# One level of Strassen's scheme for both products of an MLP, in a hybrid decoder block on one core

## The chip, the cores and the metric

The kernel runs on one core of a Trainium2 chip. The metric is device time in microseconds (us) of one execution, as the median of several runs. The core's engines are TensorE (matmuls and transposes, PE in the profile, its weight loads PEld), VectorE (DVE), ScalarE (ACT), GpSimd (POOL) and SyncE (SP), which issues most DMAs. Each engine takes its own instructions in their order and waits for others by semaphores.

## The reference, cut to what matters

One decoder layer on 1,024 positions of width 1,024, all in float32: a mixer of an SSD scan and an attention, then an MLP with squared ReLU, both with residuals. The change touches the MLP and the two norms around it.

```python
def reference(x, ...):                      # x (1, 1024, 1024)
    h = x + hybrid_mixer(rmsnorm(x, norm_mix_w), ...)
    u = square(relu(rmsnorm(h, norm_mlp_w) @ w_up))     # w_up (1024, 4096)
    h = h + u @ w_down                                   # w_down (4096, 1024)
    return rmsnorm(h, norm_final_w)
```

## The kernel before

A product of two float32 operands is made of three matmuls of the type fp32r: each operand a is split into a high part (a rounded copy) and a low part (a minus the copy), and high x high, high x low and low x high are summed in one PSUM bank. A bank holds 128 x 512 values; the pools `d`, `s`, `t` and `v` have 2, 3, 2 and 1 of them (line 105). SBUF tiles come from pools with fixed numbers of buffers (line 103); a tile that is made anew waits until the buffer's last reader is done. A scheduler sets the order on each engine, except while an engine's key is in `kept`, when its instructions keep the order in which they are written.

After the output projection, whose last part adds its result onto the residual tiles `h1` (eight of 128 x 1024), come two stages. The second norm (line 1142) takes four row tiles at a time: ScalarE squares and sums them, GpSimd makes the factor (`rstd_of`), VectorE scales, and `norm_transpose` (line 198) turns them on TensorE and splits them into `gh` (ScalarE) and `gl` (VectorE), eight tiles each, model width on partitions, all 1,024 positions.

The MLP runs over 16 chunks of two 128-wide blocks of the inner width (`FC = 2`). `mlp_up` (line 1163) loads and splits a block of `w_up` (GpSimd the high part, VectorE the low) and, for each half of the positions, sums 8 x 3 matmuls of 128 x 512 in one bank `pu`; ScalarE applies the ReLU, GpSimd squares, ScalarE and VectorE split the result into `uu`. `mlp_wd` (line 1190) splits the rows of `w_down`. `mlp_down` (line 1200) makes for each of 8 row tiles and 2 column halves 6 matmuls into a bank `pn`, which VectorE adds onto `h1`. The loop at the end calls the up products of chunk c + 1 before the down products of chunk c:

```python
    us = mlp_up(0)
    for c in range(NCH):
        wd = mlp_wd(c)
        nxt = mlp_up(c + 1) if c + 1 < NCH else None
        mlp_down(c, us, wd)
        us = nxt
```

So up and down products alternate, a chunk being 96 + 96 matmuls, and squared activations never leave SBUF. In the last chunk `final` and `store` (lines 1224 and 1243) make the final norm of each row tile as it is completed.

## Time and profile before

| | us |
|---|---|
| median of 3 runs | 1755.26 |
| lowest and highest run | 1750.23, 1757.10 |
| the profiled execution's span | 1752.7 |

The profiled execution is one run, observed by the hardware; times of single instructions are from it. Its mean granted TensorE clock is 0.986 of full speed. A page of it has six parts: busy time by engine, forty slices of the span, DMA queues, the chain of work that ended last, the costliest groups of instructions, and DMA issues. The trace behind it can be asked for a timeline, for waits, and for sums over windows. "Busy" time of matmuls overlaps, since one begins before the one ahead of it has left the array; the distance from start to start is the price of one in a stream. The MLP with the second norm stands from about 1032 to 1743 us, the final norm's rest behind it.

### The profile page before, as it was taken

The numbers are of one execution on the slowest core, as the hardware profiler recorded it, in microseconds if no ns is written. First come the engines' busy times: TensorE is split into PE (matmuls) and PEld (weight loads), VectorE is DVE, ScalarE is ACT, GpSimd is POOL, SyncE is SP. The second block draws the span as 40 slices with busy tenths as digits, with TensorE's granted clock in tenths as the row PEclk, the third lists the DMA queues.
The fourth block names the chain that finished last, engine by engine and source line by source line (L and its number), as shares of the span: only waits on it lengthen the run. The fifth ranks groups of instructions, "written<-read, shape, count | busy, mean of one in ns | idle before, by whom it ended". The sixth has DMA issues, their size and how long they took to land.

```text
span 1752.7 us, 22604 instructions
## 1 busy us (share of the span) xinstructions
PE 1696.3 (97%) x8378; PEld 1416.5 (81%) x8378; DVE 1021.6 (58%) x1959; ACT 550.6 (31%) x1277; POOL 527.1 (30%) x731
## 2 busy tenths in 40 slices
PE   7999898899999999999999999999999999999997
...
DMA packets 142134, 108.23 MB, mean 62 GB/s; under 512 B 41060, under 2 KB 125240, under 8 KB 142024
## 3 DMA queue, kind: packets, MB, share of 16 engines
...
q0 software_dynamic: 1024, 0.53, 0.1%
...
## 4 chain that ended last, share of the span: by engine, by line
PE 78%; DMA 6%; DVE 4%; ACT 3%; issue 3%; POOL 2%; POOLq 0%; DVEq 0%; ACTq 0%; SPq 0%
PE pu L85 19%; PE pn L85 19%; PE po L85 10%; PE pj_qk L85 9%; PE pj_v L85 5%; DMA eb<-cum_d 5%; PE s L85 4%; PE o L85 4%; PE tp L85 3%; PE pj_x L85 3%; ACT eb L85 2%; DVE acc_x L85 1%; PE pj_c L85 1%; PE pb L85 0%; PE pv L85 0%
## 5 line engine op out<-in xcount | busy, mean ns | idle before, releaser
L85 PE MATMUL pn<-wh_dn,uu 128*128 128x512 f32 x1024 | 318.8, 390 | 2.5 <-POOL wh_dn L85 2.4
L85 PEld LDWEIGHTS pn<-wh_dn,uu 128*128 128x128 f32 x1024 | 192.8, 188 | 43.4 <-POOL wh_dn L85 3.2
L85 DVE TENSOR_TENSOR h<-h,pn 128x512 f32<-128x512 f32 x256 | 167.7, 680 | 93.0 <-PE pn L85 92.7
L85 PE MATMUL pn<-wl_dn,uu 128*128 128x512 f32 x512 | 199.8, 391 | 0.0
L85 PE MATMUL pu<-gh,wh_up 128*128 128x512 f32 x512 | 199.7, 390 | 0.0
L85 PE MATMUL pu<-gl,wh_up 128*128 128x512 f32 x512 | 199.6, 390 | 0.0
L85 PE MATMUL pu<-gh,wl_up 128*128 128x512 f32 x512 | 199.4, 389 | 0.0
L85 ACT ACTIVATE u<-pu 128x512 f32<-128x512 f32 x64 | 38.3, 599 | 500.4 <-PE pu L85 500.4
L85 POOL TENSOR_SCALAR p<-p,rs 128x512 f32<-128x512 f32 (+2 forms) x144 | 102.8, 719 | 247.1 <-DVE rs L85 135.5
L85 PE MATMUL po<-wh_o,yy 128*128 128x512 f32 x512 | 161.8, 393 | 1.2 <-DVE k L85 1.2
L85 POOL TENSOR_TENSOR u<-u 128x512 f32<-128x512 f32 x64 | 67.9, 1060 | 256.7 <-ACT u L85 256.6
L85 ACT ACTIVATE p<-s,mx 128x512 f32<-128x512 f32 (+1 forms) x192 | 110.2, 578 | 89.8 <-DVE mx L85 69.6
L85 DVE TENSOR_TENSOR uu<-u,uu 128x512 fp32r<-128x512 f32 x64 | 44.1, 689 | 159.6 <-ACT uu L85 159.3
L85 DVE TENSOR_TENSOR pl<-tp,ph 128x512 fp32r<-128x512 f32 x192 | 105.9, 552 | 39.8 <-ACT ph L85 36.8
L85 POOL TENSOR_SCALAR wh_up<-ws_up 128x512 fp32r<-128x512 f32 x64 | 38.5, 619 | 271.6 <-DMA ws_up<-in_w_up_dram 140.0
L85 ACT CAST ph<-tp 128x512 fp32r<-128x512 f32 x192 | 91.5, 477 | 70.9 <-PE tp L85 70.5
L85 PEld LDWEIGHTS pn<-wl_dn,uu 128*128 128x128 f32 x512 | 96.6, 189 | 20.1
L85 PEld LDWEIGHTS pu<-gh,wh_up 128*128 128x128 f32 x512 | 96.1, 188 | 20.0 <-ACT gh L85 0.3
L85 PEld LDWEIGHTS pu<-gh,wl_up 128*128 128x128 f32 x512 | 96.1, 188 | 20.0 <-DVE wl_up L85 0.2
L85 PEld LDWEIGHTS pu<-gl,wh_up 128*128 128x128 f32 x512 | 96.1, 188 | 19.7
L85 PEld LDWEIGHTS po<-wh_o,yy 128*128 128x128 f32 x512 | 95.5, 188 | 20.0 <-DVE k L85 1.5
L85 DVE TENSOR_TENSOR wl_dn<-wsd,wh_dn 128x512 fp32r<-128x512 f32 x64 | 57.9, 909 | 84.3 <-POOL wh_dn L85 84.3
...
## 6 DMA issues: line engine op xcount, KB each, us to landing
ws_up<-in_w_up_dram SPq DMA_DIRECT2D x32, 512.0 KB, 4.2
wsd<-in_w_down_dram SPq DMA_DIRECT2D x32, 512.0 KB, 3.5
eb<-cum_d SPq DMA_DIRECT2D x16, 512.0 KB, 8.9
...
wso<-in_w_out_dram SPq DMA_DIRECT2D x16, 512.0 KB, 3.5
...
wsz<-in_w_in_dram SPq DMA_DIRECT2D x10, 512.0 KB, 3.7
x<-in_x_dram SPq DMA_DIRECT2D x8, 512.0 KB, 5.1
```

The source lines that it names most:

```text
L85: i = call(*args, **kw)
```

## The change

Both products of the MLP are written as 2 x 2 blocks and made by Strassen's scheme in Winograd's form: seven block products on sums and differences of blocks (s1 to s4 and a11, a12, a22 of the left operand, t1 to t4 and b11, b21, b22 of the right), whose results are summed into four output blocks. Sums are made in float32 before the split into high and low parts.

- **Second norm.** The normalised rows are four blocks: model width halves by position halves. `norm_rows` also stores `h1` to DRAM (`h1_d`), since its tiles are needed for others. The first half of the positions gives b11 and b21 and plain copies of both (`cc`); then a11 and a12 of the first pair are multiplied; the second half gives t1 to t4 and b22, made from the transposes and `cc`. TensorE's order is as written from there on.
- **Up stage.** It runs over 16 pairs of 128-wide inner blocks. `up_split` makes the seven left operands of a pair, with three sums on GpSimd and one on VectorE; ScalarE makes each high part, VectorE each low one. A product is 4 x 3 matmuls of 128 x 512. Three banks serve a pair, and two of them are read and then accumulated further: after s2 b is read, s3 is added, b is read, and so on. The four output blocks are passed through ReLU and square (ScalarE), GpSimd makes the four sums that are the left operands of the next product, and all seven go to DRAM (`uc_d`).
- **Down stage.** It begins after the whole up stage: eight chunks of two pairs, each of four slots i (row tiles i and i + 4). `down_in` loads the seven 128 x 128 blocks of a slot and pair, ScalarE makes the high part (128 x 896), GpSimd the low one (VectorE for i = 3). Inputs of a slot are asked for two slots ahead. `down_split` makes the seven right operands of a pair from `w_down`, with four sums on GpSimd. `down_mm` makes seven products of 6 matmuls; after each, VectorE adds the bank onto a quarter of `h1` or onto a sum `acc`, which the last chunk adds onto three quarters. `h1` is loaded again from DRAM before the stage.

```diff
+    h1_d = dp.tile([T, D], F32, name="h1_d")
...
+            sy.dma_start(out=h1_d[tt * P:(tt + 1) * P, :], in_=h1[tt])
...
+    def parts(o, src, low_by):
+        ac.copy(o[:, 0], src)
+        low_by.tensor_tensor(out=o[:, 1], in0=src, in1=r32(o[:, 0]), op=ALU.subtract)
+    cc = []
+    nts = norm_rows(0)
+    for k in range(HK):
+        cc.append(sb("q", [P, 2, 512], F32, f"cc{k}"))
+        for i, m in enumerate(("b11", "b21")):
+            kk = k + HK * i
+            pt = turn(nts, kk, 0)
+            quarter(m, k, pt, mlpw(kk))
+            ac.activation(cc[k][:, i, :], pt, AF.Copy, scale=mlpw(kk))
...
+    def up_prod(bank, p, m, b, first):
+        o = uop[p][m + "o"]
+        n = 0
+        for k in range(HK):
+            g = gq[b][k]
+            for x, y in ((0, 0), (0, 1), (1, 0)):
+                n += 1
+                te.matmul(
+                    bank, o[:, x, k, :], g[:, y, :], start=first and n == 1, stop=n == 3 * HK,
+                    skip_group_check=True,
+                )
...
+    uc_d = [dp.tile([P, 4, 7, P], F32, name=f"uc_d{p}") for p in range(NPAIR)]
...
+    def up_first(p):
+        a = banks[p, "a"] = ps("d", f"pu_a{p}")
+        up_prod(a, p, "a11", "b11", True)
+        t1s[p] = sb(("y", "y", "vt")[p % 3], [P, 512], F32, f"ut1_{p}")
+        ac.copy(t1s[p], a)
+    def up_second(p):
+        up_prod(banks[p, "a"], p, "a12", "b21", False)
+    def up_rest(p, between):
+        a = banks[p, "a"]
+        t1 = t1s[p]
+        st = [sb(("p", "p", "ws")[(4 * p + j) % 3], [P, 4, 2, P], F32, f"uc{p}_{j}") for j in range(4)]
...
+        b = ps("s", f"pu_b{p}")
+        up_prod(b, p, "s2", "t2", True)
+        u2 = tmp("u2")
+        ve.tensor_tensor(out=u2, in0=b, in1=t1, op=ALU.add)
+        if between is not None:
+            between()
+        ac.activation(view("a11"), v3(a), AF.Relu)
+        ac.activation(view("a11"), view("a11"), AF.Square)
+        up_prod(b, p, "s3", "t3", False)
+        u3 = tmp("u3")
+        ve.tensor_tensor(out=u3, in0=b, in1=t1, op=ALU.add)
+        c = ps("t", f"pu_c{p}")
+        up_prod(c, p, "s1", "t1", True)
+        ve.tensor_tensor(out=u3, in0=c, in1=u3, op=ALU.add)
+        up_prod(b, p, "a22", "t4", False)
+        ac.activation(u3, u3, AF.Relu)
+        ac.activation(view("a22"), v3(u3), AF.Square)
+        c21 = tmp("c21")
+        ve.tensor_tensor(out=c21, in0=b, in1=t1, op=ALU.add)
+        ac.activation(c21, c21, AF.Relu)
+        ac.activation(view("a12"), v3(c21), AF.Square)
+        up_prod(c, p, "s4", "b22", False)
+        ve.tensor_tensor(out=u2, in0=c, in1=u2, op=ALU.add)
+        act(u2, u2)
+        a21 = v3(u2)
+        gp.tensor_tensor(out=view("s3"), in0=view("a11"), in1=a21, op=ALU.subtract)
+        gp.tensor_tensor(out=view("s1"), in0=a21, in1=view("a22"), op=ALU.add)
+        gp.tensor_tensor(out=view("s2"), in0=view("s1"), in1=view("a11"), op=ALU.subtract)
+        gp.tensor_tensor(out=view("s4"), in0=view("a12"), in1=view("s2"), op=ALU.subtract)
+        for j in range(4):
+            n = min(2, 7 - 2 * j)
+            sy.dma_start(out=uc_d[p][:, :, 2 * j:2 * j + n, :], in_=st[j][:, :, 0:n, :])
...
+    up_split(0, ("a11", "a12"))
+    kept.add("t")
+    up_first(0)
+    up_second(0)
+    kept.discard("t")
+    nts = norm_rows(1)
+    pts = {}
+    kept.add("t")
...
+    for k in range(HK):
+        w1, w2 = mlpw(k), mlpw(k + HK)
+        p12 = turn(nts, k, 1)
+        c12 = sb("t", [P, 512], F32, f"c12_{k}")
+        ac.activation(c12, p12, AF.Copy, scale=w1)
+        ta = sb("ws", [P, 2, 512], F32, f"ta{k}")
+        ve.scalar_tensor_tensor(
+            out=ta[:, 0, :], in0=p12, scalar=w1, in1=cc[k][:, 0, :], op0=ALU.mult, op1=ALU.subtract
+        )
+        p22 = turn(nts, k + HK, 1)
+        ve.scalar_tensor_tensor(
+            out=ta[:, 1, :], in0=p22, scalar=w2, in1=ta[:, 0, :], op0=ALU.mult, op1=ALU.subtract
+        )
+        parts(gtile("t2", k), ta[:, 1, :], ve)
+        tb = [sb("t", [P, 512], F32, f"tb{k}_{j}") for j in range(2)]
+        ve.scalar_tensor_tensor(
+            out=tb[0], in0=p22, scalar=w2, in1=c12, op0=ALU.mult, op1=ALU.subtract
+        )
+        parts(gtile("t3", k), tb[0], ve)
+        quarter("b22", k, p22, w2)
+        parts(gtile("t1", k), ta[:, 0, :], gp)
+        gp.tensor_tensor(out=tb[1], in0=cc[k][:, 1, :], in1=ta[:, 1, :], op=ALU.subtract)
+        parts(gtile("t4", k), tb[1], gp)
+    for p in range(1, PRE):
+        up_split(p, ("a11", "a12"))
+        up_first(p)
+        up_second(p)
+    for p in range(NPAIR):
+        if p < PRE:
+            up_split(p, ("s2", "s3", "s1", "a22", "s4"))
+            up_rest(p, None)
+        else:
+            up_load(p)
+            up_split(p, ORDER)
...
+        def out(m):
+            tag = "w" if nd[0] % 22 < 6 else "hT"
+            nd[0] += 1
+            o = sb(tag, [P, 2, 512], F32R, f"do_{m}_{p}")
+            parts(o, src[m], ve)
+            dop[p, m] = o
+        out("b11")
+        add("t1", b12, b11, ALU.subtract)
+        out("t1")
+        add("t3", b22, b12, ALU.subtract)
+        out("t3")
+        add("t2", b22, src["t1"], ALU.subtract)
+        out("t2")
+        out("b21")
+        out("b22")
+        add("t4", b21, src["t2"], ALU.subtract)
+        out("t4")
...
+    def down_in(c, i):
+        for p in range(c * CP, (c + 1) * CP):
+            tag = "pq"[nu[0] % 8 // 4]
+            nu[0] += 2
+            lo = sb(tag, [P, 7, P], F32R, f"ul{p}_{i}")
+            hi = sb(tag, [P, 7, P], F32R, f"uh{p}_{i}")
+            sy.dma_start(out=r32(lo), in_=uc_d[p][:, i])
+            ac.copy(hi, r32(lo))
+            (gp if i % 4 < 3 else ve).tensor_tensor(out=lo, in0=r32(lo), in1=r32(hi), op=ALU.subtract)
+            us_in[p, i] = hi, lo
...
+    def down_mm(c, i):
+        last = c == NCH - 1
+        def prod(bank, m, b, first):
+            j = UM.index(m)
+            n, total = 0, 3 * CP
+            for p in range(c * CP, (c + 1) * CP):
+                w = dop[p, b]
+                for x, y in ((0, 0), (0, 1), (1, 0)):
+                    n += 1
+                    te.matmul(
+                        bank, us_in[p, i][x][:, j, :], w[:, y, :], start=first and n == 1,
+                        stop=n == total, skip_group_check=True,
+                    )
+        def read(bank, dst):
+            ve.tensor_tensor(out=dst, in0=dst, in1=bank, op=ALU.add)
+        h11, h12 = h1[i][:, 0:512], h1[i][:, 512:]
+        h21, h22 = h1[i + 4][:, 0:512], h1[i + 4][:, 512:]
+        nm = f"{c}_{i}"
+        ba = ps("d", f"pn_a{nm}")
+        prod(ba, "a11", "b11", True)
+        read(ba, h11)
+        bb = ps("s", f"pn_b{nm}")
+        prod(bb, "s1", "t1", True)
+        read(bb, h22)
+        bc = ps("t", f"pn_c{nm}")
+        prod(bc, "s3", "t3", True)
+        read(bc, h22)
+        prod(ba, "s2", "t2", False)
+        if c == 0:
+            acc[i] = sb("p0", [P, 512], F32, f"acc{i}")
+            ac.copy(acc[i], ba)
+        else:
+            read(ba, acc[i])
+        if last:
+            for dst in (h22, h12, h21):
+                gp.tensor_tensor(out=dst, in0=dst, in1=acc[i], op=ALU.add)
+        bd = ps("v", f"pn_d{nm}")
+        prod(bd, "a12", "b21", True)
+        read(bd, h11)
+        prod(bb, "s4", "b22", False)
+        read(bb, h12)
+        if last:
+            final(i)
+        prod(bc, "a22", "t4", False)
+        read(bc, h21)
+        if last:
+            final(i + 4)
...
+    for p in range(CP):
+        down_load(p)
+        down_split(p)
+    h1 = {}
+    for i in range(4):
+        for tt in (i, i + 4):
+            h1[tt] = sb("q", [P, D], F32, f"h1b_{tt}")
+            sy.dma_start(out=h1[tt], in_=h1_d[tt * P:(tt + 1) * P, :])
+        if i < 2:
+            down_in(0, i)
+    wfb = sb("ws", [P, D], F32, "wfb")
+    sy.dma_start(out=wfb, in_=norm_final_w.partition_broadcast(P))
+    slots = [(c, i) for c in range(NCH) for i in range(4)]
+    for n, (c, i) in enumerate(slots):
+        if c + 1 < NCH and i % 2 == 0:
+            down_load((c + 1) * CP + i // 2)
+        down_mm(c, i)
+        if n + 2 < len(slots):
+            down_in(*slots[n + 2])
+        if c + 1 < NCH and i % 2 == 1:
+            down_split((c + 1) * CP + i // 2)
```

How the instructions stand. ScalarE at the second norm, before: high parts `gh` and squares of the second half's tiles in turn (`hn4` is row tile 4, the first of the second half).

```order
L85 ACTIVATE gh4_10342<-nt_m_0_4_10410,prm_92 128x512
L85 ACTIVATE gh5_10343<-nt_m_0_5_10417,prm_92 128x512
L85 ACTIVATE gh6_10344<-nt_m_0_6_10424,prm_92 128x512
L85 ACTIVATE hn4_10438,ss_m4_10439<-h1_4_9242 128x1024
L85 ACTIVATE gh7_10345<-nt_m_0_7_10431,prm_92 128x512
L85 ACTIVATE hn5_10445,ss_m5_10446<-h1_5_9310 128x1024
```

And now: high parts, the copies `cc`, a copy of the first bank (`ut1`), and then the squares.

```order
L85 ACTIVATE g_b21_2_10424<-nt_m_0_6_10419,prm_92 128x512
L85 ACTIVATE cc2_10409<-nt_m_0_2_10410,prm_92 128x512
L85 ACTIVATE g_b11_3_10434<-nt_m_0_3_10429,prm_92 128x512
L85 ACTIVATE cc2_10409<-nt_m_0_6_10419,prm_92 128x512
L85 ACTIVATE g_b21_3_10443<-nt_m_0_7_10438,prm_92 128x512
L85 ACTIVATE cc3_10428<-nt_m_0_3_10429,prm_92 128x512
L85 COPY ut1_0_10490<-pu_a0_10477 128x512
L85 ACTIVATE cc3_10428<-nt_m_0_7_10438,prm_92 128x512
L85 ACTIVATE hn4_10504,ss_m4_10505<-h1_4_9242 128x1024
L85 ACTIVATE hn5_10512,ss_m5_10513<-h1_5_9310 128x1024
```

What moved: 17 operations instead of 7 stand ahead of the first square of the second half, and TensorE's transposes of that half, which need those squares' factors, stand behind the first pair's a11 and a12.

SP at the turn from the up to the down stage, which the kernel before does not have. `h1b` are the residual tiles loaded again, `ul0_1` the input of pair 0 for slot 1, `uc_d15` the sums of the last pair on their way to DRAM, `wsd` raw weights.

```order
L85 DMA h1b_0_13097<-h1_d_10338 128x1024
L85 DMA h1b_4_13099<-h1_d_10338 128x1024
L85 DMA h1b_1_13111<-h1_d_10338 128x1024
L85 DMA h1b_5_13113<-h1_d_10338 128x1024
L85 DMA ul0_1_13115<-uc_d0_10447 128x896
L85 DMA uc_d15_10462<-uc15_3_12932 512x1x128
L85 DMA wsd2_0_13135<-in_w_down_dram 128x1024
L85 DMA wfb_13133<-in_norm_final_w_dram 128x1024
L85 DMA ul0_0_13101<-uc_d0_10447 128x896
L85 DMA uc_d15_10462<-uc15_0_12929 512x1x256
L85 DMA uc_d15_10462<-uc15_1_12930 512x1x256
L85 DMA uc_d15_10462<-uc15_2_12931 512x1x256
```

What moved: the first input of the second pair, `ul1_0`, stands behind the last pair's stores and four residual tiles.

VectorE in a stretch of down products, before: low parts of weights (`wl`) and reads of banks onto `h1`.

```order
L85 TENSOR_TENSOR h1_4_9242<-h1_4_9242,pn0_4_0_10884 128x512
L85 TENSOR_TENSOR h1_4_9242<-h1_4_9242,pn0_4_1_10892 128x512
L85 TENSOR_TENSOR h1_5_9310<-h1_5_9310,pn0_5_0_10900 128x512
L85 TENSOR_TENSOR h1_5_9310<-h1_5_9310,pn0_5_1_10908 128x512
L85 TENSOR_TENSOR wl_up4_10967<-ws_up4_10964,wh_up4_10966 128x512 x2
L85 TENSOR_TENSOR h1_6_9378<-h1_6_9378,pn0_6_0_10916 128x512
L85 TENSOR_TENSOR h1_6_9378<-h1_6_9378,pn0_6_1_10924 128x512
L85 TENSOR_TENSOR h1_7_9416<-h1_7_9416,pn0_7_0_10932 128x512
L85 TENSOR_TENSOR h1_7_9416<-h1_7_9416,pn0_7_1_10940 128x512
```

And now, in the last slot of a chunk: `do` are low parts of the weights' operands of the next chunks, `pn` are banks.

```order
L85 TENSOR_TENSOR do_t1_7_14069<-ds_t1_7_14067,do_t1_7_14069 128x512
L85 TENSOR_TENSOR h1b_3_13129<-h1b_3_13129,pn_a2_3_14001 128x512
L85 TENSOR_TENSOR do_t3_7_14074<-ds_t3_7_14072,do_t3_7_14074 128x512
L85 TENSOR_TENSOR h1b_7_13131<-h1b_7_13131,pn_b2_3_14009 128x512
L85 TENSOR_TENSOR do_t2_7_14079<-ds_t2_7_14077,do_t2_7_14079 128x512
L85 TENSOR_TENSOR h1b_7_13131<-h1b_7_13131,pn_c2_3_14017 128x512
L85 TENSOR_TENSOR do_b21_7_14082<-wsd7_1_13936,do_b21_7_14082 128x512
L85 TENSOR_TENSOR acc3_13394<-acc3_13394,pn_a2_3_14001 128x512
L85 TENSOR_TENSOR do_b22_7_14085<-wsd7_1_13936,do_b22_7_14085 128x512
L85 TENSOR_TENSOR h1b_3_13129<-h1b_3_13129,pn_d2_3_14032 128x512
L85 TENSOR_TENSOR do_t4_7_14090<-ds_t4_7_14088,do_t4_7_14090 128x512
L85 TENSOR_TENSOR h1b_3_13129<-h1b_3_13129,pn_b2_3_14009 128x512
```

What moved: between each two reads of banks now stands a subtraction of two SBUF operands, which waits for ScalarE's high part.

## Rows read from the trace of the kernel before

**Rows 1.** The page's first part (busy us, share of the span and instructions of each engine) and TensorE's row of its 40 slices.

```profile
PE 1696.3 (97%) x8378; PEld 1416.5 (81%) x8378; DVE 1021.6 (58%) x1959; ACT 550.6 (31%) x1277; POOL 527.1 (30%) x731
...
PE   7999898899999999999999999999999999999997
```

**Rows 2.** The page's fourth part, the chain that ended last: shares by engine, then by line and tile (pu are the up products, pn the down products).

```profile
PE 78%; DMA 6%; DVE 4%; ACT 3%; issue 3%; POOL 2%; POOLq 0%; DVEq 0%; ACTq 0%; SPq 0%
PE pu L85 19%; PE pn L85 19%; PE po L85 10%; PE pj_qk L85 9%; PE pj_v L85 5%; DMA eb<-cum_d 5%; PE s L85 4%; PE o L85 4%; PE tp L85 3%; PE pj_x L85 3%; ACT eb L85 2%; DVE acc_x L85 1%; PE pj_c L85 1%; PE pb L85 0%; PE pv L85 0%
```

**Rows 3.** The page's fifth part, the matmuls of the MLP: count, busy us, mean ns of one, idle before.

```profile
L85 PE MATMUL pn<-wh_dn,uu 128*128 128x512 f32 x1024 | 318.8, 390 | 2.5 <-POOL wh_dn L85 2.4
...
L85 PE MATMUL pn<-wl_dn,uu 128*128 128x512 f32 x512 | 199.8, 391 | 0.0
...
L85 PE MATMUL pu<-gh,wh_up 128*128 128x512 f32 x512 | 199.7, 390 | 0.0
...
L85 PE MATMUL pu<-gl,wh_up 128*128 128x512 f32 x512 | 199.6, 390 | 0.0
...
L85 PE MATMUL pu<-gh,wl_up 128*128 128x512 f32 x512 | 199.4, 389 | 0.0
```

**Rows 4.** Timeline of TensorE: the first transposes of the second norm, the first up product, two matmuls of the steady stream with 21 others between them, and the last matmul (start us, us, engine, line, operation).

```profile
1031.65 3.48 PE L85 MATMUL nt_m<-ident,hn 128*128 128x128 f32 x28
...
1034.89 0.48 PE L85 MATMUL pu<-gh,wh_up 128*128 128x512 f32 x1
...
1051.02 0.39 PE L85 MATMUL pu<-gh,wh_up 128*128 128x512 f32 x1
...
1056.01 0.39 PE L85 MATMUL pu<-gl,wh_up 128*128 128x512 f32 x1
...
1742.39 0.39 PE L85 MATMUL pn<-wh_dn,uu 128*128 128x512 f32 x1
```

**Rows 5.** TensorE's waits in the window 1030 to 1753, the longest (us in total, times, longest).

```profile
PE pn L85 <- POOL wh_dn L85: 2.4, 1, 2.4
```

**Rows 6.** Windows: length, then busy us (and instructions) of TensorE, its weight loads, VectorE, ScalarE and GpSimd, then TensorE's granted clock, the DMA share and GB/s. First the whole MLP, then the stretch about the wait of rows 5.

```profile
1031.65:1742.78 711.13, 707.49 (x3137) 583.51 (x3135) 327.59 (x468) 103.31 (x181) 158.75 (x219) 1.00 0.16 49
...
1066.00:1068.00 2.00, 0.00 (x0) 0.00 (x0) 0.56 (x1) 0.00 (x0) 0.56 (x1) 1.00 0.03 4
...
1068.00:1070.00 2.00, 1.81 (x5) 1.27 (x6) 1.69 (x2) 0.00 (x0) 0.64 (x2) 0.77 0.00 0
...
1070.00:1075.00 5.00, 5.00 (x19) 3.99 (x18) 2.72 (x5) 0.00 (x0) 0.87 (x2) 0.75 0.37 105
```

**Rows 7.** The page's fifth part, the other engines' operations of the MLP: reads of a bank onto the residual, the low part of the activations, the squaring and the ReLU.

```profile
L85 DVE TENSOR_TENSOR h<-h,pn 128x512 f32<-128x512 f32 x256 | 167.7, 680 | 93.0 <-PE pn L85 92.7
...
L85 DVE TENSOR_TENSOR uu<-u,uu 128x512 fp32r<-128x512 f32 x64 | 44.1, 689 | 159.6 <-ACT uu L85 159.3
...
L85 POOL TENSOR_TENSOR u<-u 128x512 f32<-128x512 f32 x64 | 67.9, 1060 | 256.7 <-ACT u L85 256.6
...
L85 ACT ACTIVATE u<-pu 128x512 f32<-128x512 f32 x64 | 38.3, 599 | 500.4 <-PE pu L85 500.4
```

**Rows 8.** Timeline of VectorE in a stretch of down products: a subtraction with both operands in SBUF, then three reads of banks back to back.

```profile
1399.85 0.68 DVE L85 TENSOR_TENSOR wl_dn<-wsd,wh_dn 128x512 fp32r<-128x512 f32 x1
1400.46 1.87 DVE L85 TENSOR_TENSOR h<-h,pn 128x512 f32<-128x512 f32 x3
```

**Rows 9.** Timeline of GpSimd and VectorE where both work on SBUF at once (other engines' rows left out).

```profile
1081.07 1.20 POOL L85 TENSOR_SCALAR wh_up<-ws_up 128x512 fp32r<-128x512 f32 x2 [5.73 <-DMA ws_up<-in_w_up_dram]
...
1081.72 2.54 DVE L85 TENSOR_TENSOR wl_up<-ws_up,wh_up 128x512 fp32r<-128x512 f32 x2 [4.88 <-POOL wh_up L85]
...
1082.28 1.42 POOL L85 TENSOR_TENSOR u<-u 128x512 f32<-128x512 f32 x1
```

**Rows 10.** Timeline of ScalarE at the second norm: high parts of the first half, then two squares of the second half's tiles.

```profile
1032.29 4.20 ACT L85 ACTIVATE gh<-nt_m,prm 128x512 fp32r<-128x512 f32 x7 [20.27 <-PE nt_m L85]
...
1039.03 1.06 ACT L85 ACTIVATE hn<-h 128x1024 f32<-128x1024 f32 x1
...
1040.07 1.06 ACT L85 ACTIVATE hn<-h 128x1024 f32<-128x1024 f32 x1
```

**Rows 11.** Timeline of VectorE there: low parts of the first half, and the last scaled tile of the second.

```profile
1033.01 4.70 DVE L85 SCALAR_TENSOR_TENSOR gl<-nt_m,prm,gh 128x512 fp32r<-128x512 f32 x7 [0.47 <-ACT gh L85]
...
1043.02 0.75 DVE L85 TENSOR_SCALAR hn<-h,v_m 128x1024 f32<-128x1024 f32 x1 [0.71 <-POOL v_m L85]
```

**Rows 12.** Windows (columns as in rows 6): 4 us in the output projection's loads.

```profile
836.00:840.00 4.00, 2.68 (x13) 1.91 (x13) 3.29 (x13) 2.84 (x9) 0.62 (x2) 1.00 0.92 360
```

**Rows 13.** The page's sixth part, DMA issues: count, KB each, median us from issue to landing.

```profile
ws_up<-in_w_up_dram SPq DMA_DIRECT2D x32, 512.0 KB, 4.2
wsd<-in_w_down_dram SPq DMA_DIRECT2D x32, 512.0 KB, 3.5
```

**Rows 14.** Timeline of the end: VectorE's last products of the final norm and the last output DMA's issue.

```profile
1748.32 1.41 DVE L85 SCALAR_TENSOR_TENSOR fsq<-h,v_f,wfb 128x512 f32<-128x512 f32 x2 [0.71 <-POOL v_f L85]
...
1749.77 0.37 ACTq L85 DMA_DIRECT2D out_dram<-fsq  x1
```

180 lines of the change are left out of this document (92 added, 88 removed).

## Prediction

> **What bounds the kernel now.** I read the page's busy shares first, then the chain of waits, then the stretch that the change touches, by timeline and windows. TensorE is busy 97% of the span [rows 1], and the two MLP products are 38% of the chain that ended last, 19% each [rows 2]. The reader is to see that these products wait for almost nothing: 3,072 matmuls [rows 3], one wait of 2.4 us [rows 5]. So the price of one is its spacing, not its "mean ns", which overlaps its neighbours: from 1051.02 to 1056.01 there are 22 steps, 4.99 / 22 = 0.2268 us each [rows 4]. The stretch from the first transpose of the second norm (1031.65) to the end of the last matmul (1742.39 + 0.39) is 711.1 us [rows 4]. Work in it: 3,072 x 0.2268 = 696.7, and 64 transposes at (1034.89 - 1031.65) / 28 = 0.116, 7.4; together 704.1. **So 7.0 us are lost there now**, 4 of them around the one wait: no matmul in 1066 to 1068, and then a granted clock of 0.77 and 0.75, a mix of 1.2 and 2.4 GHz, costing 0.23 x 2 + 0.25 x 5 = 1.7 [rows 6]. The other engines have room: in this stretch VectorE is busy 328 of 711 us, ScalarE 103, GpSimd 159 [rows 6].
>
> **The gain.** The listing of the changed kernel shows 16 pairs x 7 x 12 = 1,344 matmuls up and 32 slots x 7 x 6 = 1,344 down, all 128x512 with a weight load each, as before. 384 fewer x 0.2268 = **87.1 us less TensorE work**. Everything else below is waiting that this work no longer covers.
>
> **Steady up stage.** A pair takes 84 x 0.2268 = 19.05. VectorE has 5 reads of banks at 0.62 (1.87 / 3) and 8 SBUF operations at 0.61 (1399.85 to 1400.46) [rows 8], 8.0 in all, and 13.3 if each of the 8 takes 2.54 / 2 = 1.27, as beside a busy GpSimd [rows 9]. ScalarE has 16 operations at about 0.60 [rows 7], 9.6. GpSimd has 7 additions at 1.06 [rows 7], 7.4, or 9.9 at 1.42 each [rows 9]. All lie under 19. A bank is read and then accumulated into again, but another product of 12 x 0.2268 = 2.72 lies between, against a read of 0.68 [rows 7] behind at most one subtraction of 1.27: covered. Without that cover each return to a bank would cost about 1.0 (read 0.68 and two handovers); that happens once each in pairs 0 and 1, where `between` is None. **+2**, bounds 0 and 6.
>
> **Start of the MLP.** Here the cover goes. ScalarE now writes, for the first four row tiles, 8 high parts and 8 plain copies `cc` and one copy of a bank before it reaches the squares of the other four tiles: from 1032.29, 17 x 0.60 = 10.2 [rows 10], then squares 1.04 apart. Its last square starts at about 1045.6, against 1040.07 now; 3.7 later (1040.07 to 1043.02 + 0.75) the last scaled tile stands [rows 10, 11]: 1049.3. Then four rounds build t1 to t4 and b22. Each has 6 ScalarE operations of 0.60 and a start-up of two VectorE operations of 0.67 [rows 11] that they wait for, about 4.5; with some pair-0 work between, 20 us. All TensorE has meanwhile is 64 transposes and the a11 and a12 products of pairs 0 and 1, whose b11 and b21 come from the first half. I put the end of s3 of pair 0 at 1074: 72 matmuls (16.3) and 64 transposes (7.4) in 42.6 us leave 19 idle. With one spell of low clock as in [rows 6], 1.7, **+21**. Bounds: 12 (the four rounds run at ScalarE's pace alone, 24 x 0.60 = 14.4, and start where the squares now end) and 27 (half clock through both idle stretches).
>
> **Between up and down.** Before, down products of a chunk followed up products of the next, and no stage ended. Now the first down product needs inputs that come back from DRAM, and the order shows what stands ahead of them. The four input tiles take the buffers of the last pair's sums. After the last up product at T: read 0.68, ReLU, a cast, square 3 x 0.60, three GpSimd sums 3 x 1.06, then on GpSimd a weight sum that waits for its own load, and the fourth sum: T + 8. The write to DRAM, 3.5 as a 512 KB load takes [rows 13], T + 11.7; the load into the freed tile, T + 15; high part of 896 columns 0.60 x 896 / 512 = 1.05, low part on GpSimd 1.06 x 896 / 512 = 1.85: T + 18. A second path: on SP, three 512 KB residual tiles (released only in the last product), three more loads and a write stand ahead of the first input, 3.7 MB; at 360 GB/s, the most that I read in 4 us [rows 12], 10 us. The first half of the inputs can start the products earlier. I take 16, and 1.7 of clock: **+18**, bounds 8 (inputs meet old tiles) and 24.
>
> **Steady down stage.** A slot is 42 matmuls, 9.53; a chunk four slots, 38.1. VectorE per chunk: 28 reads at 0.62, 14 weight subtractions, 2 input subtractions of 896. Alone: 17.4 + 14 x 0.61 + 2 x 1.07 = 28.1. But the order puts all 14 in the last slot of a chunk and the first of the next, one between each two reads: 14 x 1.23 = 17.2 of 19.05 with nothing to slow them. GpSimd has in those two slots 4 input subtractions (1.85) and some 6 sums (1.06), 13.8 of 19.05. What one costs beside the other, the rows show: two subtractions 2.54 while GpSimd's addition takes 1.42 instead of 1.06 [rows 7, 9]. Stepped row by row at 0.9 a subtraction and 0.61 a read, the first read in the second of these slots ends 14.6 after the first slot began; the product that goes into that bank again is due at 9.53 + 3 x 1.36 = 13.6, so TensorE waits some 1.1. Nine subtractions stand ahead of it, so at 1.15 each it waits 3.3. Inputs run on two buffers: load 3.5, casts, two subtractions of 1.85 to 2.5 on GpSimd, 8 to 10 us against 9.53. I take 2.5 for each of 7 boundaries, **+17.5**, nearer [rows 9] than [rows 8], since GpSimd is busy 70% there; bounds 0 and 6 each. In the last chunk two input loads stand on SP behind output stores that wait for the final norm: **+5**, bounds 0 and 8.
>
> The Trainium skill has a rule against this part. Its page "SBUF — State Buffer", section "Who interferes with whom", says that a VectorE instruction with two SBUF inputs and a GpSimd instruction that reads SBUF shut each other out for the whole instruction. The trace agrees: both reach 2.54 and 1.42 in [rows 9], and PSUM reads, with one SBUF input, stay at 0.68 [rows 7]. By it a subtraction can wait out a whole input subtraction of 1.85; where that held for every instruction, the time would be that of the second rival below.
>
> **Tail.** After the last matmul come 9.9 us now (1742.8 to 1752.7) [rows 4, 14]; the new final norm has the same steps with fewer tiles waiting: 0, bounds -2 and +2. Elsewhere nothing moves but eight residual stores and four weight splits inside the output projection, where TensorE does not wait for VectorE now: 0.
>
> **How the numbers follow.** Against the profiled execution: -87.1 - 7.0 + 2 + 21 + 18 + 17.5 + 5 = -30.6, so 1752.7 - 30.6 = 1722. The median of the runs is 2.6 above the profiled span: **1725**. All low bounds together (0 + 12 + 8 + 0 + 0 - 2 = 18) would give 1679, all high ones (6 + 27 + 24 + 42 + 8 + 2 = 109) 1770. Chance of a time near the forecast, 1700 to 1742: 0.60.
>
> **Rivals.**
> 1. *The waits are absorbed.* Raw tiles and sums are fetched a pair ahead, so the boundary slots may cost 0.5 each, the turn 10 and the start 15: 15 + 10 + 4 + 2 = 31, -63, with the 2.6 a time of 1692. For it: GpSimd's sums stand two slots early in the order. Against: ScalarE's 17 operations at the start have no slack. 0.17.
> 2. *VectorE and GpSimd become the bound of the down stage, and the kernel is slower.* If VectorE and GpSimd take turns throughout, a chunk costs 28.1 + 6 x 1.85 + 8 x 1.06 = 47.7 in place of 38.1, +9.6 for 8 chunks = 77 instead of 22.5: -94.1 + 41 + 77 = +24, a time of 1779. It decides from 6.6 us a chunk ((94.1 - 41) / 8), and from 7.7 it is slower by over 0.5%. For it: reads stand in line behind the subtractions. Against: the reads themselves don't slow beside GpSimd [rows 7]. 0.09.
> 3. *The inputs come late in every slot.* If load, casts and two subtractions (up to 11 us) exceed the slot by 1.5, 32 x 1.5 = 48 in place of 22.5: -5, a time of 1750. For it: each load also waits in SP's line behind weight loads. Against: 1.4 MB per slot is 150 GB/s, and 360 were moved in [rows 12]. 0.14.
> That the products are not fewer is excluded by the listing.
>
> Range: 1688 to 1757, which leaves out the slower case and some of the absorbed one. 0.5% (about what a measurement of this kernel can tell from no change) is 8.8 us: faster 0.77 (forecast and first rival), same 0.14 (third), slower 0.09 (second).
>
> **What would show it.** In the profile after: spacing of up products still 0.227 and no waits in the middle of the up stage; a TensorE gap of 15 to 20 us spread over the first 42 us of the MLP, with ScalarE busy throughout; one gap of some 16 us between the last up and the first down product, ended by an input tile; in the down stage waits at chunk boundaries, released by VectorE's reads, and subtractions of 0.9 to 1.2. Wrong would be: a subtraction near 0.7 (rival 1), TensorE waiting in every slot for inputs (rival 3), or VectorE busy nine tenths of the down stage (rival 2).

## The result: slower by 0.9%

| | before | after |
|---|---|---|
| median of 4 runs, us | 1754.03 | 1767.05 |
| lowest and highest | 1750.23, 1757.10 | 1766.85, 1774.25 |
| span of the profiled execution | 1752.7 | 1765.0 |

The ratio is 1.0086, with a 95% interval of 1.0063 to 1.0109. The forecast was 1725, with a range to 1757.

**The profile after.** First the page's busy share of TensorE, its row of slices and the chain (they answer to [rows 1, 2]):

```profile
PE 1632.2 (92%) x7994; PEld 1349.6 (76%) x7994; DVE 1211.0 (69%) x2082; ACT 763.7 (43%) x1610; POOL 779.0 (44%) x788
...
PE   7999898899999999999999968999999599888896
...
PE 63%; DVE 11%; DMA 8%; issue 5%; ACT 5%; POOL 4%; SPq 0%; POOLq 0%; DVEq 0%; ACTq 0%
```

TensorE is 64 us less busy, but its share of the span fell from 97% to 92%, and its share of the chain from 78% to 63%. TensorE's waits from 1030 on (they answer to [rows 5]; us in total, times, longest):

```profile
PE pn_a L85 <- POOL ul L85: 26.7, 16, 5.3
PE pn_a L85 <- DVE h1b L85: 16.5, 10, 2.8
PE pn_a L85 <- ACT uh L85: 14.3, 3, 9.5
```

All three stand before products into the bank pn_a, which opens a down slot and comes back in its middle. `ul` is a low part of the inputs, `h1b` a read onto the residual, `uh` a high part. Windows then show where the time went (they answer to [rows 6]; columns: length, then busy us and instructions of TensorE, weight loads, VectorE, ScalarE, GpSimd, then the granted clock, DMA share, GB/s):

```profile
1027.12:1091.62 64.50, 45.75 (x198) 36.01 (x196) 46.07 (x55) 39.88 (x70) 32.32 (x27) 0.87 0.15 48
1091.62:1366.34 274.72, 274.72 (x1213) 227.29 (x1211) 158.29 (x185) 138.29 (x230) 139.08 (x101) 1.00 0.51 161
1366.34:1410.05 43.71, 23.83 (x85) 17.67 (x85) 38.11 (x32) 17.86 (x29) 40.34 (x24) 0.73 0.64 233
1429.09:1446.68 17.59, 13.23 (x44) 9.72 (x42) 17.59 (x16) 3.18 (x5) 14.09 (x8) 0.81 0.33 112
1446.68:1475.24 28.56, 28.56 (x128) 23.65 (x126) 21.49 (x29) 12.26 (x19) 11.99 (x7) 1.00 0.34 115
1429.09:1703.99 274.90, 242.53 (x1009) 192.54 (x1008) 229.78 (x263) 87.41 (x127) 151.14 (x81) 0.97 0.35 119
1703.99:1753.80 49.81, 44.35 (x169) 34.05 (x167) 26.66 (x40) 18.83 (x39) 36.11 (x39) 0.90 0.35 119
```

In order: the start of the MLP; the rest of the up stage, where TensorE never pauses (1,212 matmuls in 274.72, 0.2267 each); the turn to the third down slot; slot 0 of chunk 1; slots 1 to 3 of chunk 1, again without a pause; chunks 1 to 6 together; chunk 7. So chunk 1 loses its time in its first slot alone. Over chunks 1 to 6, 35.2 of the 46.4 us lost lie in the first slot of a chunk, the rest in the second and third, none in the fourth. With TensorE's work taken off (0.2267 a matmul, 7.4 for the transposes) each term of the sum can be read:

| term | forecast | after |
|---|---|---|
| 384 matmuls fewer | -87.1 | -87.1 |
| losses of before, gone | -7.0 | -7.0 |
| start of the MLP and steady up stage | 21 + 2 | 64.5 - 37.3 = 27.2, and 0 |
| turn | 18 | 43.7 - 19.05 = 24.7 |
| chunks 1 to 6 | 6 x 2.5 = 15 | 274.9 - 228.5 = 46.4 |
| chunk 7 with its boundary | 2.5 + 5 | 49.8 - 38.1 = 11.7 |
| after the last matmul | 0 | +1.3 |
| ahead of the MLP | 0 | -4.5 |
| sum | -30.6 | 12.7 (measured 12.3) |

The -4.5 lies in code that the change leaves alone: the first transposes start at 1027.12 where they stood at 1031.65 [rows 4]. It is no effect of the change that I can show; in the twelve kernels of the experiments they start anywhere from 1026.5 to 1032.0. Without that row and the one above it, the stages exceed the forecast by 46 us, of which 31 are in the six middle chunks.

The same windows also split the loss by kind. TensorE's idle time is a window's length less its busy time: 18.8 at the start, 19.9 at the turn, 32.4 in chunks 1 to 6 and 5.5 in chunk 7. The rest is TensorE busy longer than its work takes at 0.2267 a matmul: 8.4, 4.8, 14.0 and 6.3, together 33.5, where the forecast had two spells of low clock of 1.7 each. Outside chunks 1 to 6 the idle time is 44.1 us for a forecast of 44.5 (19 + 2, 16, and 2.5 + 5).

**One boundary, row by row.** TensorE in slot 0 of chunk 1 (start us, us, operation, count, idle before and what ended it):

```profile
1432.67 0.50 PE L85 MATMUL pn_a<-do_b,ul 128*128 128x512 f32 x1 [2.28 <-POOL ul L85]
...
1434.62 1.05 PE L85 MATMUL pn_c<-do_t,uh 128*128 128x512 f32 x2
...
1435.90 1.05 PE L85 MATMUL pn_c<-do_t,uh 128*128 128x512 f32 x2
...
1439.45 0.74 PE L85 MATMUL pn_a<-do_t,uh 128*128 128x512 f32 x2 [2.07 <-DVE h1b L85]
...
1440.96 1.05 PE L85 MATMUL pn_d<-do_b,uh 128*128 128x512 f32 x2
```

The slot takes 17.59 us for 9.52 of work. TensorE waits 2.28 for a low part of GpSimd's and 2.07 for VectorE's read of the bank that s2 x t2 wants back. Between and behind the waits the matmuls stand 0.43 apart (1434.62 to 1435.90, three in 1.28) where 0.227 is usual: about half the clock. The slot's window shows a granted clock of 0.81, and a window over 1434.20 to 1437.40 alone one of 0.50. So 4.35 of the 8.07 us lost are waits, and 3.7 are slower matmuls behind them. VectorE there:

```profile
1424.36 2.03 DVE L85 TENSOR_TENSOR do_t<-ds_t,do_t 128x512 fp32r<-128x512 f32 x1
...
1428.90 1.78 DVE L85 TENSOR_TENSOR do_t<-ds_t,do_t 128x512 fp32r<-128x512 f32 x1
...
1431.20 1.96 DVE L85 TENSOR_TENSOR do_b<-wsd,do_b 128x512 fp32r<-128x512 f32 x1
...
1439.32 1.39 DVE L85 TENSOR_TENSOR do_b<-wsd,do_b 128x512 fp32r<-128x512 f32 x1
...
1446.26 0.68 DVE L85 TENSOR_TENSOR do_b<-wsd,do_b 128x512 fp32r<-128x512 f32 x1
```

A weight subtraction takes 1.96 to 2.03 beside a low part of GpSimd's, 1.39 to 1.78 beside a weight sum, and 0.68 while GpSimd is idle (1446.26). The reads stand between these subtractions. GpSimd there:

```profile
1421.99 1.29 POOL L85 TENSOR_TENSOR ds_t<-wsd,ds_t 128x512 f32<-128x512 f32 x1 [11.67 <-DVE do_t L85]
...
1430.10 2.52 POOL L85 TENSOR_TENSOR ul<-ul,uh 128x896 fp32r<-128x896 f32 x1
...
1432.57 1.75 POOL L85 TENSOR_TENSOR ds_t<-wsd,wsd 128x512 f32<-128x512 f32 x1
```

The low part that TensorE waits for is made from 1430.10 to 1432.62, though ScalarE had its high part ready at 1426.75. Ahead of it in GpSimd's line stand weight sums that wait for tiles which VectorE's subtractions still read: 11.67 us at 1421.99, then 0.69 and 0.63. The two engines' lines thus hold each other up. In chunks 1 to 6 the groups are:

```profile
L85 DVE TENSOR_TENSOR do_t<-ds_t,do_t 128x512 fp32r<-128x512 f32 x48 | 69.0, 1437 | 3.9 <-ACT do_t L85 3.9
...
L85 DVE TENSOR_TENSOR do_b<-wsd,do_b 128x512 fp32r<-128x512 f32 x35 | 48.8, 1394 | 0.0
...
L85 POOL TENSOR_TENSOR ds_t<-wsd,ds_t 128x512 f32<-128x512 f32 x22 | 29.9, 1358 | 64.1 <-DVE do_t L85 60.5 <-PE pn_c L85 3.5
...
L85 POOL TENSOR_TENSOR ul<-ul,uh 128x896 fp32r<-128x896 f32 x37 | 88.1, 2390 | 44.7 <-ACT uh L85 44.6
```

`do_t` are the weight subtractions on sums, `do_b` those on raw blocks; all 83 together take 1.42 in the mean. TensorE's 32.3 us of waits in these chunks are 18.9 for low parts and 13.4 for VectorE's reads.

The slower matmuls are of two kinds. Chunks 3 to 5 run at a granted clock of 1.00, and still TensorE is busy 118.55 for 114.3 of work there, some 0.3 for each of its 13 waits:

```profile
1521.54:1658.09 136.55, 118.55 (x505) 93.43 (x504) 113.67 (x133) 45.13 (x67) 79.29 (x43) 1.00 0.37 127
```

In chunks 1, 2 and 6 it is busy 9.7 longer than its work; there the granted clock is 0.93 to 0.96.

### The profile page after: what moved, and what is told of

It is laid out like the page before. It is cut to its first block, busy times and chain, and to the rows that moved or that the text cites. A ratio compares the mean times of both kernels' runs of the same rounds, so it can differ in the third digit from the quotient of the medians.

```text
span 1765.0 us, 22987 instructions
## 1 busy us (share of the span) xinstructions
PE 1632.2 (92%) x7994; PEld 1349.6 (76%) x7994; DVE 1211.0 (69%) x2082; ACT 763.7 (43%) x1610; POOL 779.0 (44%) x788
## 4 chain that ended last, share of the span: by engine, by line
PE 63%; DVE 11%; DMA 8%; issue 5%; ACT 5%; POOL 4%; SPq 0%; POOLq 0%; DVEq 0%; ACTq 0%
PE po L85 9%; PE pj_qk L85 8%; PE pu_b L85 7%; PE pj_v L85 5%; DMA eb<-cum_d 5%; PE pu_c L85 5%; PE pu_a L85 4%; PE s L85 4%; PE o L85 3%; PE tp L85 3%; PE pj_x L85 3%; PE pn_a L85 3%; PE pn_b L85 2%; DVE do_t L85 2%; PE pn_c L85 2%
## 5 line engine op out<-in xcount | busy, mean ns | idle before, releaser
L85 POOL TENSOR_TENSOR ul<-ul,uh 128x896 fp32r<-128x896 f32 x48 | 112.9, 2361 | 54.0 <-ACT uh L85 53.7
L85 DVE TENSOR_TENSOR pl<-tp,ph 128x512 fp32r<-128x512 f32 x192 | 105.9, 553 | 38.1 <-ACT ph L85 34.9
L85 PE MATMUL pj_qk<-hh,wl_qk 128*128 128x512 f32 x256 | 106.2, 415 | 0.0
L85 PE MATMUL pj_qk<-hl,wh_qk 128*128 128x512 f32 x256 | 105.9, 414 | 0.0
L85 PE MATMUL pj_qk<-hh,wh_qk 128*128 128x512 f32 x256 | 103.4, 404 | 0.0
L85 PE MATMUL s<-k,q 68*128 68x512 f32 (+7 forms) x384 | 101.9, 347 | 1.1 <-ACT p L85 0.9
L85 PE MATMUL po<-wl_o,yy 128*128 128x512 f32 x256 | 100.6, 393 | 0.0
L85 PE MATMUL pu_b<-g_t,uo_s 128*128 128x512 f32 x384 | 93.9, 394 | 4.0 <-DVE uu L85 4.0
L85 PE MATMUL tp<-ident,p 128*128 128x128 f32 x576 | 95.2, 273 | 1.2 <-POOL p L85 1.2
L85 PE MATMUL pu_a<-g_b,uo_a 128*128 128x512 f32 x384 | 94.5, 396 | 1.4 <-ACT ut L85 1.4
L85 DVE TENSOR_TENSOR do_t<-ds_t,do_t 128x512 fp32r<-128x512 f32 x64 | 91.6, 1433 | 5.6 <-ACT do_t L85 5.5
```

The source lines that it names most:

```text
L85: i = call(*args, **kw)
```

## Experiments

Three theories. **Lock**: VectorE's subtractions (two SBUF operands) and GpSimd's instructions take turns, and these longer durations are the loss. **Burst**: the loss comes from the order; 14 splits stand in two slots, and half of them belong to the chunk after next. **Inputs**: load, casts and two low parts take longer than a slot. VectorE's order in slot 3 of chunk 0 shows what the burst is (`do_t1_3` is the split of block t1 of pair 3, `pn_a0_3` the bank a of chunk 0, slot 3):

```order
L85 TENSOR_TENSOR do_t1_3_13433<-ds_t1_3_13431,do_t1_3_13433 128x512
L85 TENSOR_TENSOR h1b_3_13129<-h1b_3_13129,pn_a0_3_13364 128x512
L85 TENSOR_TENSOR do_b11_4_13587<-wsd4_0_13457,do_b11_4_13587 128x512
L85 TENSOR_TENSOR h1b_7_13131<-h1b_7_13131,pn_b0_3_13372 128x512
L85 TENSOR_TENSOR do_t3_3_13438<-ds_t3_3_13436,do_t3_3_13438 128x512
L85 TENSOR_TENSOR h1b_7_13131<-h1b_7_13131,pn_c0_3_13380 128x512
L85 TENSOR_TENSOR do_t2_3_13443<-ds_t2_3_13441,do_t2_3_13443 128x512
L85 TENSOR_TENSOR do_b21_3_13446<-wsd3_1_13298,do_b21_3_13446 128x512
L85 TENSOR_TENSOR do_t1_4_13592<-ds_t1_4_13590,do_t1_4_13592 128x512
```

Pair 3 is of chunk 1 and urgent; pair 4 is of chunk 2 and needed 38 us later. Tiles of both come free in the same slot, and so both are split there, between the reads.

**e1, the order alone.** `side` holds what stands behind each of a slot's seven reads; `a` and `b` are the next chunk's pairs, and `convert` (CV = 3) makes the high and low parts of the next slot's inputs:

```diff
+            if i == 1:
+                down_load(b)
+                jobs[b] = down_jobs(b)
+                side.update({k + 1: [jobs[a][1][k]] for k in range(4)})
+            if i == 2:
+                jobs[b][0]()
+                side.update({k - 3: [jobs[a][1][k]] for k in range(4, 7)})
+                side[5] = [jobs[b][1][0]]
+            if i == 3:
+                side.update({k: [jobs[b][1][k]] for k in range(1, 6)})
+                late = [jobs[b][1][6]]
...
+            side[CV] = [lambda s=slots[n + 1]: convert(*s)] + side.get(CV, [])
```

> The same instructions as in the changed kernel, but in the down stage (all chunks but the last) VectorE, ScalarE and GpSimd keep an order written by hand: the seven weight splits of a chunk's first pair stand in slots 1 and 2 of the chunk before, those of its second pair from the end of slot 2 to the beginning of slot 0, one behind each read of a bank, and a slot's inputs are cast in the middle of the slot ahead. Now a chunk of 38.1 takes 45.0 to 46.3 (chunks 1 to 6). Burst theory (14 splits stand in two slots, 7 of them not needed for another 38 us): chunks fall to 38 to 40, some 40 us in all, a time of about 1727. Lock theory (VectorE and GpSimd stretch each other wherever they meet, in any order): chunks stay above 43, a time of 1750 to 1760. Input theory (load, casts and two subtractions take longer than a slot): the waits for ul stay, 1 to 2 us in two slots of four, chunks 41 to 42, a time of about 1742.

Measured: 1727.56 us (1726.27 to 1728.77), ratio 0.9848 (0.9832 to 0.9865). Chunks 1 to 6, as a window and four groups:

```profile
1433.87:1663.71 229.84, 228.82 (x1009) 189.15 (x1008) 208.57 (x266) 91.34 (x133) 154.83 (x85) 1.00 0.44 144
...
L85 DVE TENSOR_TENSOR do_t<-ds_t,do_t 128x512 fp32r<-128x512 f32 x50 | 69.9, 1400 | 2.7 <-ACT do_t L85 2.7
...
L85 DVE TENSOR_TENSOR do_b<-wsd,do_b 128x512 fp32r<-128x512 f32 x36 | 30.0, 834 | 0.0
...
L85 POOL TENSOR_TENSOR ds_t<-wsd,ds_t 128x512 f32<-128x512 f32 x24 | 33.3, 1390 | 0.9
...
L85 POOL TENSOR_TENSOR ul<-ul,uh 128x896 fp32r<-128x896 f32 x37 | 86.9, 2370 | 73.3 <-ACT uh L85 72.9 <-DMA ul<-uc_d 0.2
```

They take 229.8 for 228.5 of work. The burst theory gave the time to the microsecond. What matters more: the subtractions on sums are as slow as in the changed kernel (1.40 against 1.44), GpSimd's low parts too (2.37 against 2.39), and VectorE is busy 91% of the stretch. So these slow instructions fit into the chunk, and neither engine was the bound of the stage. Not everything stayed slow, though: the subtractions on raw blocks fell from 1.39 to 0.83, which makes 1.16 in the mean of all weight subtractions, and GpSimd's sums in the group shown wait 0.9 in all, where they waited 60.5 for VectorE. The order written by hand covers ScalarE's casts and GpSimd's sums and low parts too, so e1 doesn't say which engine's order counts.

**e2 and e3, less for GpSimd; e4, no splits.**

In this order:

```diff
- gp.tensor_tensor(out=src[m], in0=x, in1=y, op=op)
+ src[m] = x
...
- (gp if i % 4 < 3 else ve).tensor_tensor(out=lo, in0=r32(lo), in1=r32(hi), op=ALU.subtract)
+ if i % 4 == 3:
+     ve.tensor_tensor(out=lo, in0=r32(lo), in1=r32(hi), op=ALU.subtract)
...
- w = dop[p, b]
+ w = dop[p % CP, b]
```

> Leaves out the weight sums of the down stage (64 GpSimd additions): raw blocks are split in their place, by the same ScalarE and VectorE instructions. Lock theory: the weight subtractions, now 1.43 us in the mean, fall to about 1.0, since GpSimd has 6 input subtractions a chunk left, and chunks 1 to 6 to about 41. Input theory: the low parts no longer stand behind sums on GpSimd, TensorE's waits for ul (26.7 us in the MLP) fall below 10, those for reads stay at 16; chunks about 43. Burst theory: the 14 splits stay in two slots, chunks about 44.

> Leaves out GpSimd's 48 subtractions for the low parts of the down inputs (three slots of four; the low factor is then the whole value). GpSimd keeps the weight sums. Lock theory: weight subtractions fall to 1.0 or below, chunks 1 to 6 to 39 to 41. Input theory: the waits for ul vanish and those for reads stay, chunks 42 to 43. Burst theory: 14 splits at 0.7 to 1.0 and 14 reads fill two slots, chunks about 41.

> Splits the down weights of chunk 0 alone and uses them in all chunks (leaves out the loads, sums and splits of 14 pairs). Burst theory and lock theory: chunks 1 to 6 take 38.1 to 38.5, some 46 us less. Input theory: the inputs still come late in some slots, chunks 41 to 42. The turn between the stages and the start stay as they are (24.7 and 27.2 us lost) under all three.

Measured 1740.93, 1724.23 and 1720.37 (one run each). The subtractions `do_t` of e2, then those of e3, each in its chunks 1 to 6:

```profile
L85 DVE TENSOR_TENSOR do_t<-wsd,do_t 128x512 fp32r<-128x512 f32 x47 | 50.4, 1071 | 3.9 <-ACT do_t L85 3.9
```

```profile
L85 DVE TENSOR_TENSOR do_t<-ds_t,do_t 128x512 fp32r<-128x512 f32 x49 | 48.5, 989 | 4.2 <-ACT do_t L85 4.2
```

| kernel | a chunk over 38.1 | TensorE's waits in six chunks | do_t, us | do_b, us | GpSimd's ul, us |
|---|---|---|---|---|---|
| after | 7.7 | 32.3 | 1.44 | 1.39 | 2.39 |
| e1, order by hand | 0.2 | 1.0 | 1.40 | 0.83 | 2.37 |
| e2, no sums | 3.1 | 12.9 | 1.07 | 1.25 | 2.21 |
| e3, no low parts on GpSimd | 1.5 | 5.6 | 0.99 | 0.96 | |
| e4, no splits | 0.0 | 0 | | | 2.13 |
| e9, low parts on VectorE | 2.4 | 7.0 | 0.87 | 0.80 | |

e4 and e1 throw the input theory out: with the same input loads, casts and low parts in each slot, chunks 1 to 6 wait for nothing in e4, which leaves the weight loads out too, and 1.0 us in e1, which keeps them. In e2 the waits for low parts fall from 18.9 to 3.8, since no sums stand ahead of them, and those for reads from 13.4 to 9.1. e3 is 0.8 a chunk without chunk 1. So taking work from GpSimd helps too, in the old order. And e2 against e1 shows what the order is worth where the stretch is equal: weight subtractions of 1.15 in the mean cost 3.1 a chunk in the old order, and 1.16 cost 0.2 in the new one.

**e9, the lock, with nothing left out.** One line of the changed kernel:

```diff
- (gp if i % 4 < 3 else ve).tensor_tensor(out=lo, in0=r32(lo), in1=r32(hi), op=ALU.subtract)
+ ve.tensor_tensor(out=lo, in0=r32(lo), in1=r32(hi), op=ALU.subtract)
```

> The changed kernel with one line different: all low parts of the down inputs are VectorE's (GpSimd made 48 of 64), the order of the splits as the scheduler puts it. Lock theory (a GpSimd subtraction of 896 columns and a VectorE subtraction keep each other out, so the burst of 14 splits lasts too long only beside them): chunks 1 to 6 fall from 45.0 to 46.3 to about 39 to 41, a time of about 1735, although VectorE has 6.5 us more work a chunk. Burst theory alone (too many VectorE instructions in two slots, whatever GpSimd does): the two low parts more in such a slot make it worse, chunks of 46 or more, a time of 1767 or above.

Measured: 1734.31 us (1731.28 to 1735.43), ratio 0.9886 (0.9870 to 0.9903). Chunks 1 to 6:

```profile
1434.15:1676.90 242.75, 235.49 (x1009) 187.35 (x1008) 228.56 (x302) 87.48 (x127) 60.00 (x44) 1.00 0.41 135
...
L85 DVE TENSOR_TENSOR do_t<-ds_t,do_t 128x512 fp32r<-128x512 f32 x48 | 41.8, 871 | 1.2 <-ACT do_t L85 0.9
```

VectorE makes 36 subtractions more in this stretch, and yet its busy time is 228.6, against 229.8 in the changed kernel: what it took over it won back, since its weight subtractions fell from 1.44 to 0.87 on sums and from 1.39 to 0.80 on raw blocks. A chunk takes 40.5, as the lock theory said. So neither the order nor the lock is the cause by itself: the loss needs both, a burst whose instructions are stretched. e9 doesn't show the lock by itself, since its low parts also no longer stand behind GpSimd's sums; how much of the gain is that queue was not tried. Taking the low parts from GpSimd gives (7.7 - 2.4) / 7.7 = 69% of a chunk's loss back, the order 97%.

**e5 and e10, the turn**, on e1's order. e5 gives the first inputs other buffers and puts their loads first; e10 also writes chunk 0's splits between the reads of the last up pair and writes that pair's sums to DRAM behind the loads:

```diff
- tag = "pq"[nu[0] % 8 // 4]
+ tag = "qp"[nu[0] % 8 // 4]
- tag = "w" if nd[0] % 22 < 6 else "hT"
+ tag = "hT" if nd[0] % 22 < 16 else "w"
```

> On the order of e1: the inputs of the first down slot take buffers of the tiles t3 (free three products before the up stage ends) in place of those of the last pair's sums, their loads stand ahead of the residual tiles on SP, the low parts of the first two slots are VectorE's, and the first 16 weight splits take tiles that the up stage frees early. Line theory (the turn's 22 to 25 us are the wait for GpSimd's sums, their writes and the loads behind them): the turn falls to 6 to 10 lost, a time of about 1713. Rival, the splits of the first two pairs (14 at up to 2.5 us beside GpSimd) end last in any case: the turn stays above 16, a time of 1722 or more.

> On the order of e1, a second try at the turn: the 14 splits of chunk 0 are written between the reads of the last up pair, the inputs of slots 0 and 1 take up-stage tiles that come free before that pair ends, the low parts of slot 1 stand inside slot 0 and not ahead of its reads, and the last pair's sums are written to DRAM behind these loads. The turn loses 24.7 us now and 20.5 in e5. If the splits and VectorE's line were what was left in e5: 6 to 9 lost, a time of about 1712. If the loads themselves set it (inputs, weights and residual tiles, 5 MB at 360 to 400 GB/s): 14 or more.

e5 took 1720.85 (one run, as for e6, e7, e10 and e11) and loses 20.5 in the turn: the rival's number came out, but its reason accounts for about half. The first slot's product began at once; then it waited 3.52 and 4.56 for weight splits, as the rival said, and 8.80 in a wait that I had made: low parts of slot 1, whose inputs were loaded late, stood ahead of the slot's reads in VectorE's line (VectorE, then TensorE):

```profile
1387.82 2.29 DVE L85 TENSOR_TENSOR ul<-ul,uh 128x896 fp32r<-128x896 f32 x2 [3.89 <-ACT uh L85]
...
1390.77 1.22 PE L85 MATMUL pn_a<-do_t,uh 128*128 128x512 f32 x2 [8.80 <-DVE h1b L85]
```

e10 took 1719.34 and loses 10.6 in the turn. But its last up pair now ends 7.0 us later than in e1 (347.6 from the first transpose, against 340.6), since reads of up banks stand behind stretched splits, and the first down product still waits 5.82 (VectorE, VectorE, TensorE, GpSimd):

```profile
1361.20 5.16 DVE L85 TENSOR_TENSOR do_t<-ds_t,do_t 128x512 fp32r<-128x512 f32 x3
...
1367.95 0.68 DVE L85 TENSOR_TENSOR uu<-pu_b,ut 128x512 f32<-128x512 f32 x1
...
1382.43 1.22 PE L85 MATMUL pn_a<-do_b,uh 128*128 128x512 f32 x2 [5.82 <-ACT uh L85]
...
1381.63 1.27 POOL L85 TENSOR_TENSOR uc<-uc,uu 128x512 f32<-128x512 f32 x1 [9.28 <-ACT uu L85]
```

So 14.1 - 7.0 = 7.1 is what is won. The wait that is left in the turn is not the lock's: GpSimd is idle for 9.28 us ahead of 1381.63 (last row), and five splits take about 0.6 each. In the written order they stand ahead of the last read of an up bank, and that bank's ReLU stands ahead of the input casts on ScalarE.

**e6 and e11, the last chunk**, on e1's order (the second line is e6's, the third e11's):

```diff
- gp.tensor_tensor(out=dst, in0=dst, in1=acc[i], op=ALU.add)
+ ve.tensor_tensor(out=dst, in0=dst, in1=acc[i], op=ALU.add)
...
+ ve.tensor_tensor(out=dst, in0=dst, in1=ba, op=ALU.add)
```

> On the order of e1: in the last chunk the 12 additions of the common sum to the residual go from GpSimd to VectorE. GpSimd theory (its two low parts of 2.3 and three additions of 1.3 a slot, with the norm's work, exceed a slot of 9.53, and VectorE's reads wait in line behind them): the last chunk, 11.6 us over its 38.1 in e1, falls to 1 to 4 over, a time of about 1719. Rival, input loads stand behind the output stores on SP: it stays at 8 or more over.

> On the order of e1, a second try at the last chunk: the common sum of chunks 0 to 6 is added to the residual in chunk 6's slots by GpSimd, chunk 7 reads its bank three times in place of one read and three additions of SBUF tiles, and the final norm of a slot's rows stands in the slot behind it, so that no read waits in VectorE's line for a scale. The last chunk takes 49.7 in e1, 11.6 over. If those additions and that line made it: 1 to 4 over, a time of about 1719. If the norm's own chain makes it: 8 or more over.

e11 also gives VectorE one of the two low parts of each of chunk 7's first three slots, where GpSimd had both, and keeps the written order in chunk 7.

e6 took 1726.94; chunk 7 is 10.3 over, against 11.6 in e1. e11 took 1723.50; chunk 7 is 3.6 over, but chunk 6, which lost nothing in e1, is 5.6 over. In e6 the rival's number came out, but not its reason: of chunk 7's waits 6.9 us are for VectorE's reads, 1.0 for a low part, none for a load. The additions moved (in e11 to GpSimd in chunk 6), and the waits moved with them. e8 (below) shows it on VectorE: three additions beside GpSimd's two low parts, and a product of the norm that takes 1.75 beside GpSimd's, with reads behind it:

```profile
1668.27 5.03 DVE L85 TENSOR_TENSOR h1b<-h1b,acc 128x512 f32<-128x512 f32 x3
...
1678.59 1.75 DVE L85 SCALAR_TENSOR_TENSOR fsq<-h1b,v_f,wfb 128x512 f32<-128x512 f32 x1 [0.72 <-POOL v_f L85]
...
1667.51 4.64 POOL L85 TENSOR_TENSOR ul<-ul,uh 128x896 fp32r<-128x896 f32 x2 [6.45 <-DMA ul<-uc_d]
```

**e7, the start**, on e1's order:

```diff
+            if i:
+                ve.tensor_scalar_mul(cc[k][:, i, :], pt, mlpw(kk))
...
+        if k == 0:
+            up_split(1, ("a11", "a12"))
+            up_first(1)
+        if k == 1:
+            up_second(1)
```

> On the order of e1: at the start of the MLP the first two products of pair 1 stand between the second half's transposes (after rounds 0 and 1) in place of behind them, and 4 of the 8 plain copies cc go from ScalarE to VectorE. The start loses 27.2 us now. Cover theory (TensorE idles for want of work in its own order while VectorE and ScalarE build t1 to t4): 24 products of 0.227 move into the idle time and 4 copies of 0.60 leave ScalarE's line, so 19 to 22 lost. Rival, the last of t1 to t4 set the end of the start whatever TensorE does meanwhile: 25 or more lost, since the moved products are then missing behind.

It took 1725.74. From the first transpose to the end of the up stage pass 339.2 us, as in the changed kernel, against 340.6 in e1. Kernels that leave this stretch alone take 339.2 to 343.9, so no gain is shown, and the rival's number holds. VectorE's low parts of t1 to t4 still take 1.75 beside GpSimd's, as in:

```profile
1059.28 1.75 DVE L85 TENSOR_TENSOR g_t<-tb,g_t 128x512 fp32r<-128x512 f32 x1
```

**e8 and e12, together.** e8 is e1 with e5, e6 and e7; e12 is e1 with e10 and e11.

> e5, e6 and e7 together on the order of e1. If each removes its own wait: 1727.6 less 14, 8 and 6, about 1700, a ratio of 0.969 to the kernel before. If they share a cause (one engine's line that stays full), less: above 1710.

> e10 and e11 together on the order of e1: 1727.6 less 16 and 8, about 1704, a ratio of 0.971 to the kernel before, if each stage's wait is its own; above 1715 if the one moves into the other.

e8: 1721.66 (1720.33 to 1723.79), ratio 0.983 (0.9814 to 0.9846). e12: 1718.37 (1714.67 to 1723.19), ratio 0.9803 (0.9781 to 0.9824), the lowest median here, though its interval overlaps e8's and its runs take in e10's single one. Both beat the kernel before and the changed one. Both fall short of the 1700 and 1704 that I expected: in e8 the turn loses 21.0 and chunk 7 11.2; in e12 the turn 10.7 and chunks 6 and 7 8.8, and the last up pair ends 8.6 later than in e1.

## Why the prediction was wrong

- *Matmuls.* Right: 2,688 at 0.2267, nothing lost in the steady up stage (bounds 0 and 6).
- *Chunk boundaries: the step that failed.* "so at 1.15 each it waits 3.3", and "I take 2.5 for each of 7 boundaries", with 6 as the upper bound. Measured: 7.7 in the mean of six (6.9 to 8.2). The wait that this step priced, for VectorE's reads, is 13.4 / 6 = 2.2 a chunk. What it put at nothing is the rest. First, TensorE's wait for GpSimd's low parts, 18.9 / 6 = 3.2 a chunk: I set the inputs' 8 to 10 us against a slot of 9.53 and stopped there, but in GpSimd's line a low part stands behind sums that wait for VectorE's burst. Second, the slower matmuls behind each wait, (46.4 - 32.3) / 6 = 2.3 a chunk: I gave the start and the turn a spell of low clock each, and the boundaries none.
- *Two sizes under it.* That 2.2 lies near 2.5 is in part luck: VectorE goes on while TensorE waits for a low part, and the subtraction that I stepped at 0.9 to 1.15 takes 1.42 in the mean of all, 1.44 for those on sums (median 1.47, longest 2.60). The 1.06 and 1.42 of [rows 7, 9] that I took for GpSimd's additions are of a squaring; a weight sum takes 1.27 at the least in the changed kernel. And the low part, 1.85 worked out from that squaring, takes 2.09 at the least and 2.39 in the mean.
- *The rule that I gave too little weight.* Two subtractions took 5.03 beside two low parts of together 4.99:

```profile
1371.56 1.71 POOL L85 TENSOR_TENSOR uc<-uc,uu 128x512 f32<-128x512 f32 x1
...
1379.92 4.99 POOL L85 TENSOR_TENSOR ul<-ul,uh 128x896 fp32r<-128x896 f32 x2
...
1380.43 5.03 DVE L85 TENSOR_TENSOR do_b<-wsd,do_b 128x512 fp32r<-128x512 f32 x2
```

  In these rows each lasts as long as the GpSimd instruction beside it. I had priced a part of that. The Trainium skill, "SBUF — State Buffer", section "Who interferes with whom", says that such a pair shut each other out for the whole instruction, and these rows agree (2.5 in place of 0.68).
- *Rival 2* came nearest: its turning point was 6.6 a chunk, its price 9.6, and 7.7 was measured. But its reason, that the engines become the bound, is not what the runs show. In e1 the same instructions, most of them as slow as before, fit into the chunk. The loss is in the order times the stretch.
- *Rival 3* is refuted by e4 and e1; the late inputs of the changed kernel are low parts behind weight sums, not a slot too short.
- *Turn.* 24.7 for 18, above the bound of 24: 19.9 of waits for 16, and 4.8 of slower matmuls for 1.7. The path was the one I named: the first product waits for GpSimd's sums, then for low parts behind them, and then (3.11) for the second pair's input, which comes back from DRAM:

```profile
1375.96 1.22 PE L85 MATMUL pn_a<-do_b,uh 128*128 128x512 f32 x2 [9.46 <-ACT uh L85]
...
1382.48 0.80 PE L85 MATMUL pn_a<-do_b,ul 128*128 128x512 f32 x1 [5.31 <-POOL ul L85]
```

  GpSimd's sums took 1.7 in place of 1.06 and the low parts 2.5 in place of 1.85; for the waits that is the same misprice.
- *Start.* 27.2 for 21 and 2, where the start's own bound was 27. The waits are 18.8, no more than the 19 and 2 that I gave them (the 42.6 us to 1074 in my working are 42.35); the excess is TensorE busy 45.75 for 37.3 of work, 8.4 where I put 1.7, at a granted clock of 0.87 in the mean. The path of the waits was another than I said: I took ScalarE as the pace of the four rounds, 4.5 us each with the wait for VectorE. The rounds stand 5.77 apart (the first `ta` of two of them below), and VectorE is full, busy 23.23 of the 24 us from 1046 to 1070: its low parts take 1.75 beside a GpSimd one of 1.71.

```profile
1049.29 1.75 DVE L85 TENSOR_TENSOR g_t<-tb,g_t 128x512 fp32r<-128x512 f32 x1
...
1051.62 0.74 DVE L85 SCALAR_TENSOR_TENSOR ta<-nt_m,prm,cc 128x512 f32<-128x512 f32 x1
...
1057.38 0.74 DVE L85 SCALAR_TENSOR_TENSOR ta<-nt_m,prm,cc 128x512 f32<-128x512 f32 x1
...
1048.78 1.71 POOL L85 TENSOR_TENSOR g_t<-ta,g_t 128x512 fp32r<-128x512 f32 x1
```

- *Last chunk.* 11.7 for 7.5: 5.5 of waits, under the forecast, and 6.3 of slower matmuls at a granted clock of 0.90, for which I had nothing. I named output stores ahead of input loads. In the changed kernel one input load is issued at 1724.22, behind four output stores, and TensorE waits 1.70 for that input's high part and 1.43 for its low part. In e6, e8 and e11 the waits are for VectorE's and GpSimd's lines. How much the stores cost was not tried by itself.
- *What would show it.* I wrote that subtractions near 0.7 or VectorE busy nine tenths would decide between rivals. It was busy 84% (229.8 of 274.9) in the slow order and 91% in the fast one, so a mean busy share doesn't tell.
